# Order of small matmuls, two transposed blocks and the closing normalization in a one-core block kernel

## Chip, cores and metric

The kernel runs on one core of one Trainium2 chip. The metric is the device time of one execution in microseconds (us), as a median of several runs. The engines are TensorE (PE in the profile, PEld for its weight loads), VectorE (DVE), ScalarE (ACT), GpSimd (POOL) and SyncE (SP, which issues most DMAs). Data lies in SBUF, matmul results in PSUM, inputs and scratch in DRAM.

## What is computed

One layer of a network on 256 tokens of width 2048, in fp32: a feed-forward stage, a mixer and a second feed-forward stage, each between two normalizations and added to the running value. The mixer is the part that matters here:

```python
def _hybrid_mixer(u, w_in, ...):
    p = u @ w_in
    z_a, z_b, g_a, g_b = jnp.split(p, IN_SPLITS, axis=-1)
    y_a = _rwkv7_branch(z_a, ...) @ w_proj_a
    y_b = _pool_branch(z_b, pool_w, pool_scale) @ w_proj_b
    m = jax.nn.sigmoid(g_a) * y_a + jax.nn.sigmoid(g_b) * y_b
    return m @ w_out

def reference(x, ...):
    h = x
    f = _swiglu(_rmsnorm(h, ln_ffn1_pre[l]), ffn1_gate[l], ffn1_up[l], ffn1_down[l])
    h = h + MACARON_WEIGHT * _rmsnorm(f, ln_ffn1_post[l])
    mx = _hybrid_mixer(_rmsnorm(h, ln_mix_pre[l]), w_in[l], ...)
    h = h + _rmsnorm(mx, ln_mix_post[l])
    f = _swiglu(_rmsnorm(h, ln_ffn2_pre[l]), ffn2_gate[l], ffn2_up[l], ffn2_down[l])
    h = h + MACARON_WEIGHT * _rmsnorm(f, ln_ffn2_post[l])
    return h
```

`_rwkv7_branch` is a recurrence over the 256 tokens with 16 heads of 64. The kernel computes it in four chunks of 64 tokens for each half of the heads.

## The kernel before

**Products.** A product is done with the 256 tokens as two halves of 128 rows and 512 columns of the weight at a time (a block). Each fp32 factor is split into a high part H (rounded by ScalarE) and a low part L (the rest, by VectorE); a product is three matmuls of 128x128 by 512 columns (`mm3`): H·H, H·L and L·H. Weights come by DMA into `w32`, and are split into `wH` and `wL`, five buffers each. The activations must lie with their width along the partitions, so a result of one product is transposed before the next: `transpose_split` does it with four TensorE transposes of 128x128 for each half and block (tile `tr`), cast by ScalarE into `xH` and subtracted by VectorE into `xL`. The feed-forward stages use another way, `turn` and `carry`: VectorE turns 32x32 squares of the block into `T1`, SyncE writes `T1` to DRAM (`cx`), waits, and reads it back in four pieces with the squares put in their places (`x32`); the split then reads `x32`.

**The order.** Every operation is first recorded by `Plan`, with a cost. `simulate` then plays the five engines with these costs and writes out the order in which each engine gets its instructions. TensorE's operations belong to streams: `main` (the large products), `side` (transposes) and `chain` (the recurrence). At each step TensorE takes the first stream of chain, side, main whose next operation can go. The recurrence's matmuls are small and use the array in other shapes (64x128, 128x64, 64x64, 32x32); `cfg` tells the shape, and a change of it has a planned price (`SWITCH`). `deadlines` puts neighbouring chain operations of one shape into a `run`, and `whole` lets a run begin only when the operands of its first `RUN` = 16 operations are there and enough PSUM buffers are free; once begun, single operations of the run may go. All the results of chain and side share four PSUM buffers (`pt`). Results that matter: `pA` (products of AR and BK), `pB` (transposes of BK), then `pM`, `pX` and, for each chunk, `pU`, `pSa`, `pS`, `pY`; last `pg`.

**The mixer's end.** `MIX_ORDER` lists the main products; its last entries are the second half's recurrence `c1` and the gates `A0` to `A3`. The recurrence leaves `yT` (two halves, `yH` and `yL`). Then w_proj_a follows: `pairs` does the first two blocks of 512 columns together, first with the four row groups of the first half of `yT`, then with those of the second, in four PSUM banks; `gemm_tok` does the two others one by one. The evacuation `ev_pa` multiplies a block by its gate (`sga`), adds the other branch (`mb`, read back from DRAM) and calls `transpose_split` into `mT`. Then `down` does w_out, 2048 columns in two pairs of blocks f and l; some row groups (quads) are done by a scheme with seven products in place of eight, on the row groups of `mT[0]`. `OUT_QUADS` says how many quads, and after how many ordinary steps the first may come.

**The end of a stage.** `post` takes the four column blocks of the last product of a stage. For the last block (c = 3) and each half it makes the sum of squares (`sumsq`, ScalarE, tile `junk`), the factor of the normalization (`norm`: VectorE, then a power on GpSimd, tile `rs`), the product with the gain (`scale`, VectorE, tile `fg`), and then the four results. Sum of squares and product read the same PSUM buffer, and the planner does not let two engines read one buffer at once.

Of the kernel before, what the change touches and what calls it, by code (L numbers as in the profile page):

```python
# [15 lines left out]
ALU = mybir.AluOpType  # L16
# [10 lines left out]
NKW = W // P  # L27
# [16 lines left out]
AHEAD = 40000.0  # L44
EASE = 2.0
GATE_QUADS = [0, 0] + [3, 4] * 4 + [3]
OUT_QUADS = ((2, 2, 1.0), (2, 1, 1.0))
DOWN_QUADS = ((8, 1, 2.4), (8, 1, 1.7))
SCRATCH = 1024
SPARE = 1  # L50
HOLD = 3e5
Z_DMA = "k0 v0 k1 v1 r1"
POOL_DMA = [True, True]
MIX_ORDER = "p0 p1 l0 k0 m0 v0 m1 r0 m2 c0 B1 m3 k1 b0 b1 v1 r1 c1 B2 b2 B3 b3 A0 A1 A2 A3"
# [10 lines left out]


class TileInfo:
    __slots__ = ("tag", "left", "slot", "seq", "writes", "reads", "psum", "dl", "home", "lock")


class Engine:
# [10 lines left out]
LAND = 1600.0  # L82
SWITCH = 170.0
RUN = 16
TABLES = {AF.Exp: (0,), AF.Sigmoid: (2,), AF.Tanh: (0, 2, 18), AF.Silu: (18,)}
IN_ORDER = ("w32", "wH", "wL", "hH", "hL")


class Plan:

    def __init__(s, tc):
        s.tc, s.real = tc, tc.nc
        nc = s.real
        s.ops, s.tiles, s.tags, s.masks = [], {}, {}, {}
        s.order = {}
        s.shadow = bacc.Bacc("TRN2", target_bir_lowering=False, num_devices=1)
        s.clk, s.stream, s.lag, s.dl0 = 0.0, "main", 12000.0, None
        s.vector = Engine(s, "DVE", nc.vector)
        s.scalar = Engine(s, "ACT", nc.scalar)
        s.tensor = Engine(s, "PE", nc.tensor)  # L100
        s.gpsimd = Engine(s, "POOL", nc.gpsimd)
        s.sync = Engine(s, "SP", nc.sync)
# [8 lines left out]
    def tile(s, shape, dt, tag, name, pool, bufs):  # L111
        s.tags[tag] = bufs
        t = s.track(s.shadow.dram_tensor(name, tuple(shape), dt).ap(), tag)
        s.tiles[name].home = pool, list(shape), dt
        return t

    def region(s, ap):
# [32 lines left out]
    def add(s, eng, name, fn, a, k):  # L150
        o = Op()
        o.eng, o.fn, o.a, o.k = eng, fn, a, k
        o.i, o.nom, o.stream, o.lag = len(s.ops), s.clk, s.stream, s.lag
        o.preds, o.succs, o.tiles, o.new = set(), [], [], []
        aps = [(f"a{j}", x) for j, x in enumerate(a)] + list(k.items())
        aps = [(n, x) for n, x in aps if isinstance(x, bass.AP)]
        outs = [n for n, _ in aps if n in ("out", "accum_out")] or ["a0"]
        w = [x for n, x in aps if n in outs]
        r = [x for n, x in aps if n not in outs]
        if name == "memset":  # L160
            w, r = [a[0]], []
        s.cost(o, name, w, r, k)
        seen = set()
        for aplist, wr in ((r, False), (w, True)):
            for ap in aplist:
                g = s.region(ap)
                if g is None:
                    continue
                i, p0, p1, m = g
                if id(i) not in seen:  # L170
                    seen.add(id(i))
                    o.tiles.append(i)
                    i.left += 1
                for q0, q1, n, x, _ in i.writes:
                    if q0 < p1 and p0 < q1 and n & m and x is not o:
                        o.preds.add(x.i)
                if wr:
                    for q0, q1, n, x, _ in i.reads:
                        if q0 < p1 and p0 < q1 and n & m and x is not o:
                            o.preds.add(x.i)  # L180
                    for lst in (i.writes, i.reads):
                        lst[:] = [e for e in lst if not (p0 <= e[0] and e[1] <= p1
                                                         and e[2] & m == e[2])]
                    i.writes.append((p0, p1, m, o, None))
                else:
                    key = (p0, p1, m, eng, s.stream)
                    if eng == "PE":
                        i.reads[:] = [e for e in i.reads if e[4] != key]
                    i.reads.append((p0, p1, m, o, key))
        o.psum = [i for i in o.tiles if i.psum]  # L190
        s.ops.append(o)
        if eng == "PE" and s.stream == "main":
            s.clk += o.pace
        return o
# [46 lines left out]
    def deadlines(s):  # L241
        for o in s.ops:
            for p in o.preds:
                s.ops[p].succs.append(o)
        soon = {}
        for o in s.ops:
            if o.stream == "chain":
                soon[o.i] = max([soon[q] + s.ops[q].dur + SYNC for q in o.preds if q in soon
                                 and s.ops[q].nom == o.nom] or [0.0])
        idx, tip, run = {}, {}, []  # L250
        for o in s.ops:
            g = max([idx.get(q, -1) if s.ops[q].eng == "PE" else tip[q] for q in o.preds]
                    or [-1])
            tip[o.i] = g
            o.run = None
            if o.eng != "PE" or o.stream != "chain":
                continue
            idx[o.i] = len(idx)
            far = max([tip[q] for q in o.preds if s.ops[q].eng != "PE"] or [-1])
            if not run or run[-1].cfg != o.cfg or far >= idx[run[0].i]:  # L260
                run = []
            run.append(o)
            o.run = run
        for o in reversed(s.ops):
            d = o.nom + (0.0 if o.eng == "PE" else o.lag) + soon.get(o.i, 0.0) * EASE
            for x in o.succs:
                if o.eng == "PE" and x.eng == "PE":
                    continue
                e = x.dl - o.dur - SYNC - (2500 if o.nbytes else 0)
                if e < d:  # L270
                    d = e
            o.dl = d

    def simulate(s):
        s.deadlines()
        ops = s.ops
# [36 lines left out]
        def whole(o):  # L313
            if o.run is None or o.run is held:
                return True
            for x in o.run[:RUN]:
                for q in x.preds:
                    y = ops[q]
                    if y.eng != "PE" and (y.start is None or y.end + SYNC > now):
                        return False  # L320
            need = {id(i) for x in o.run[:RUN] for i in x.psum if i.slot is None}
            return len(need) <= len(slots["pt"])

        def go(o):
# [44 lines left out]
        while done < len(ops):  # L369
            moved = True  # L370
            while moved:
                moved = False
                for e in engines:
# [12 lines left out]
                    if e == "PE":  # L386
                        for st in rank:
                            q = streams[st]
                            if q and ready[q[0].i] and can(q[0]) and whole(q[0]):
                                held = q[0].run  # L390
                                go(q.popleft())
                                moved = True
                                break
                        continue
                    skipped = []
# [73 lines left out]
class Block:  # L469
# [272 lines left out]
            return x.rearrange("p (b k t) -> p k b t", k=4, t=32)  # L742
        return x.rearrange("p (i h k t) -> p k h i t", i=4, h=2, k=4)

    def carry(s, T1, T):
        v = s.carry_raw(T1)
        T.extend(s.new_T(1))
        for h in range(2):
            H, L = [t.rearrange("p k (h i t) -> p k h i t", h=2, i=4)[:, :, h] for t in T[-1]]
            s.split(v[:, :, h], H, L)  # L750

    def sumsq(s, src, acc):
# [139 lines left out]
class Kernel(Block):  # L892
# [156 lines left out]
    def post(s, gpost, fac, resid, emit, reload):  # L1049
# [10 lines left out]

        def norm(h, r):
            r2 = s.small(1, "rt2", bufs=2)
            nc.vector.tensor_scalar(out=r2, in0=ss[h][:, 3:4], scalar1=kf,
                                    scalar2=part[h], op0=ALU.mult, op1=ALU.add)
            nc.gpsimd.tensor_tensor(out=r, in0=r2, in1=s.mhalf[:, :1], op=ALU.pow)

        def ev(c, h, ps):
            if h == 0 and c % 2 == 0:
# [6 lines left out]
            if c == 3:  # L1075
                r = s.small(1, "rs", bufs=8)
                with s.set(lag=100.0):
                    s.sumsq(ps, ss[h][:, c:c + 1])
                    norm(h, r)
                    scale()  # L1080
                    for q in range(4):
                        o = cc_(fg[h], q)
                        nc.vector.scalar_tensor_tensor(out=o, in0=o, scalar=r,
                                                       in1=resid(h, q), op0=ALU.mult,
                                                       op1=ALU.add)
                        emit(h, q, o)
# [179 lines left out]
    def mixer(s, prm, uT, rs, resid, emit, gpost, reload):  # L1266
# [104 lines left out]
        mbs = {}  # L1371

        def ev_pa(c):
            def ev(h, ps):
                if h == 0:
                    mbs[c] = s.unit((P, 2, 512), F32, "mb")
# [1 line left out]
                sg = sga[c][:, h]  # L1378
                nc.vector.tensor_tensor(out=sg, in0=ps, in1=sg, op=ALU.mult)
                nc.vector.tensor_tensor(out=sg, in0=sg, in1=mbs[c][:, h], op=ALU.add)  # L1380
                s.transpose_split(sg, mT, c, h)
            return ev
        for x in MIX_ORDER.split():
            n = int(x[1])
# [10 lines left out]
                    chain(n)  # L1395
            else:
                {"B": gb_g, "b": pb_g, "A": ga_g}[x[0]](n)
        s.pairs(prm["w_proj_a"], (0, 512), at_a, NKW, 4, (ev_pa(0), ev_pa(1)))
        for c in range(2, 4):
            s.gemm_tok(prm["w_proj_a"], c * 512, at_a, NKW, ev_pa(c))  # L1400
        s.down(prm["w_out"], s.T_at(mT), NKD, s.post(gpost, 1.0, resid, emit, reload), mT,
               [], OUT_QUADS)
# [475 lines left out]
```

## Time and profile before

| | us |
|---|---|
| median of 3 runs | 2022.7 |
| lowest, highest | 2022.35, 2023.87 |
| the profiled execution, its own time | 2022.16 |
| its span, first to last instruction | 2020.2 |
| TensorE matmuls busy in it | 2002.1 |
| VectorE, ScalarE busy | 1750.4, 1185.9 |

The rows that the prediction shows are of three kinds. A row of the time order has the start in us from the beginning of the span, the length in us, the engine, the line of the code (455 for every operation, since a helper issues them all), the operation, the tile written, the tiles read, shapes and a count of equal instructions that follow each other; in brackets the idle time ahead of it and what ended it. A matmul's length is its time through the pipeline; matmuls start closer together than that. A small fp32 matmul of the chain stands as two in the trace. A row of the chain of waits has start, length and what the time went to. A row by groups has the count, the busy time, the mean in ns, and the idle time ahead.

### The profile page before, as it was taken

The page shows a single profiled execution, that of the slowest core. Times are in us where ns is not written, and L with a number is a line of the kernel's source. Part 1 is how long each engine was busy: PE and PEld are TensorE (multiplying, and loading weights), DVE is VectorE, ACT ScalarE, POOL GpSimd, SP SyncE. Part 2 cuts the span into 40 slices and gives each one's busy share as a digit, 9 for nine tenths or more (in the row PEclk, how much of TensorE's full clock was granted, in tenths as well). Part 3 has the DMA queues.
Part 4 walks back from the last instruction along what each step waited for, and adds up shares of the span by engine and source line. Part 5 has one row for each costly group of instructions (what it writes and reads, how often), then busy time and mean ns, then how long its engine had stood idle before and what let it go on. Part 6 is the DMA issues. An engine that isn't in the chain of part 4 may idle for free.

```text
span 2020.2 us, 28152 instructions
## 1 busy us (share of the span) xinstructions
PE 2002.1 (99%) x9835; PEld 1652.7 (82%) x9835; DVE 1750.4 (87%) x2284; ACT 1185.9 (59%) x1592; POOL 80.7 (4%) x148
## 2 busy tenths in 40 slices
PE   9999999999999999999999999999999999999998
PEld 7888888888888888887888788888888888788886
DVE  8999999999988758897868779798999999898885
ACT  7555656565555556764846455575555665655552
POOL 0000000000001110001200110010000000000000
PEclk9999999999999999999999999999999999999999
DMA  7788888886667677756475475667888888876673
GB/s 266 239 261 268 281 268 275 266 282 219 214 203 258 214 249 206 221 162 209 143 233 179 145 261 197 200 209 241 273 273 276 269 270 273 280 227 203 208 253 133
DMA packets 254054, 469.87 MB, mean 233 GB/s; under 512 B 20559, under 2 KB 42201, under 8 KB 253913
## 3 DMA queue, kind: packets, MB, share of 16 engines
q1 hardware_dynamic: 247737, 447.63, 68.5%
q0 software_dynamic: 5888, 19.93, 2.8%
q8 instruction: 77, 1.26, 0.3%
q14 instruction: 64, 0.52, 0.1%
q10 hardware_dynamic: 288, 0.52, 0.1%
HBM read 444.40 MB, written 23.59 MB: 232 GB/s over the span
## 4 chain that ended last, share of the span: by engine, by line
PE 79%; DVE 9%; DMA 6%; issue 3%; ACT 2%; SPq 1%; DVEq 0%; ACTq 0%; POOLq 0%
PE l L455 26%; PE f L455 23%; PE mm L455 22%; PE p L455 5%; DVE wL L455 4%; DMA w<-in_ffn_gate_dram 2%; DMA x<-cx 2%; DVE t L455 1%; ACT wH L455 1%; SPq L455 1%; DMA w<-in_ffn_up_dram 1%; PE tr L455 1%; DVE w L455 0%; PE pY L455 0%; DMA x<-in_x_dram 0%
## 5 line engine op out<-in xcount | busy, mean ns | idle before, releaser
L455 ACT CAST wH<-w 128x1024 fp32r<-128x1024 f32 (+2 forms) x722 | 746.7, 1046 | 632.4 <-DVE w L455 170.8
L455 DVE TENSOR_TENSOR wL<-w,wH 128x1024 fp32r<-128x1024 f32 (+2 forms) x722 | 863.2, 1210 | 167.6 <-ACT wH L455 163.4
L455 PE MATMUL l<-wL,xH 128*128 128x512 f32 x784 | 305.7, 390 | 0.8 <-DVE wL L455 0.7
L455 PE MATMUL l<-wH,xH 128*128 128x512 f32 x784 | 305.4, 390 | 0.0
L455 PE MATMUL l<-wH,xL 128*128 128x512 f32 x784 | 305.3, 389 | 0.0
L455 PE MATMUL mm<-wL,xH 128*128 128x512 f32 (+1 forms) x672 | 261.6, 389 | 0.0
L455 PE MATMUL mm<-wH,xH 128*128 128x512 f32 (+1 forms) x672 | 261.1, 389 | 0.0
L455 PE MATMUL mm<-wH,xL 128*128 128x512 f32 (+1 forms) x672 | 260.7, 388 | 0.0
L455 PE MATMUL f<-wH,xH 128*128 128x512 f32 x664 | 258.5, 389 | 0.0
L455 PE MATMUL f<-wL,xH 128*128 128x512 f32 x664 | 258.4, 389 | 0.0
L455 PE MATMUL f<-wH,xL 128*128 128x512 f32 x664 | 258.4, 389 | 0.0
L455 DVE TENSOR_TENSOR t<-w,w 128x1024 f32<-128x1024 f32 (+1 forms) x160 | 162.1, 1013 | 14.6 <-DMA w<-in_ffn_down_dram 8.0
L455 PEld LDWEIGHTS l<-wL,xH 128*128 128x128 f32 x784 | 147.2, 188 | 32.5 <-DVE wL L455 2.2
L455 PEld LDWEIGHTS l<-wH,xH 128*128 128x128 f32 x784 | 147.2, 188 | 30.6
L455 PEld LDWEIGHTS l<-wH,xL 128*128 128x128 f32 x784 | 147.2, 188 | 30.1
L455 PEld LDWEIGHTS mm<-wL,xH 128*128 128x128 f32 x672 | 126.4, 188 | 25.2 <-DVE wL L455 0.4
L455 PEld LDWEIGHTS mm<-wH,xH 128*128 128x128 f32 x672 | 126.3, 188 | 24.9
L455 PEld LDWEIGHTS mm<-wH,xL 128*128 128x128 f32 x672 | 126.2, 188 | 24.8 <-DVE xL L455 0.4
L455 PEld LDWEIGHTS f<-wH,xH 128*128 128x128 f32 x664 | 124.6, 188 | 26.0
L455 PEld LDWEIGHTS f<-wL,xH 128*128 128x128 f32 x664 | 124.6, 188 | 25.9
L455 PEld LDWEIGHTS f<-wH,xL 128*128 128x128 f32 x664 | 124.6, 188 | 25.8
L455 DVE TENSOR_TENSOR wL<-t,wH 128x1024 fp32r<-128x1024 f32 x98 | 119.0, 1214 | 3.0 <-ACT wH L455 2.8
(307 smaller groups left out, 2697.4 us busy)
## 6 DMA issues: line engine op xcount, KB each, us to landing
w<-in_w_in_dram SPq DMA_DIRECT2D x128, 512.0 KB
w<-in_ffn_up_dram SPq DMA_DIRECT2D x114, 512.0 KB
w<-in_ffn_gate_dram SPq DMA_DIRECT2D x112, 512.0 KB
w<-in_ffn_down_dram SPq DMA_DIRECT2D x112, 512.0 KB
w<-in_ffn_gate_dram SPq DMA_DIRECT2D x190, 256.0 KB
w<-in_ffn_up_dram SPq DMA_DIRECT2D x186, 256.0 KB
w<-in_ffn_down_dram SPq DMA_DIRECT2D x128, 256.0 KB
cx<-T SPq DMA_DIRECT2D x29, 512.0 KB
```

The costliest lines, as they stand in the source:

```text
L455: ins = o.fn(*[real(x) for x in o.a], **{n: real(x) for n, x in o.k.items()})
```

## The change

Four edits. In the planner, a run ends after 16 operations or when the kind of the result (the name of the PSUM tile) changes, `whole` asks for the whole run, and a new function `soon` makes TensorE hold back other work while the array is in a small shape and the next run of the chain can start within `STAY` = 400 planned ns. In the mixer, the first two blocks of w_proj_a are turned by VectorE and carried through DRAM instead of being transposed by TensorE; the four blocks are done one by one, without `pairs`; and w_out's first quad comes one step later. In `post`, the product of the last block is recorded as following the first step of `norm`, so the sum of squares comes first.

```diff
-OUT_QUADS = ((2, 2, 1.0), (2, 1, 1.0))
+OUT_QUADS = ((2, 3, 1.0), (2, 1, 1.0))
+MIX_DMA = 2
+STAY = 400.0
@@ Plan.add
+        if s.behind is not None:
+            o.preds.add(s.behind.i)
@@ Plan.deadlines
-            if not run or run[-1].cfg != o.cfg or far >= idx[run[0].i]:
+            if not run or run[-1].cfg != o.cfg or far >= idx[run[0].i] or len(run) == RUN \
+                    or run[-1].psum[0].kind != o.psum[0].kind:
                 run = []
@@ Plan.simulate
-            for x in o.run[:RUN]:
+            for x in o.run:
...
+        def soon(o):
+            for x in o.run or [o]:
+                for q in x.preds:
+                    y = ops[q]
+                    if y.eng != "PE" and (y.start is None or y.end + 305.0 > now + STAY):
+                        return False
+            need = {id(i) for x in o.run or [o] for i in x.psum if i.slot is None}
             return len(need) <= len(slots["pt"])
...
+                            if q and st == "chain" and cfg != (0, 0) and can(q[0]) and soon(q[0]):
+                                break
@@ Kernel.post
-                    norm(h, r)
-                    scale()
+                    with s.set(behind=norm(h, r)):
+                        scale()
@@ Kernel.mixer, ev_pa
-                s.transpose_split(sg, mT, c, h)
+                if c >= MIX_DMA:
+                    s.transpose_split(sg, mT, c, h)
+                    return
+                if not h:
+                    T1.append(s.unit(p="T1"))
+                s.turn(T1[0], h, sg)
+                if h:
+                    s.carry(T1[0], mT, c)
@@ Kernel.mixer
-        s.pairs(prm["w_proj_a"], (0, 512), at_a, NKW, 4, (ev_pa(0), ev_pa(1)))
-        for c in range(2, 4):
+        for c in range(4):
             s.gemm_tok(prm["w_proj_a"], c * 512, at_a, NKW, ev_pa(c))
```

`norm` returns its first VectorE instruction, a tile keeps its kind (its name without the number), and `carry` takes the place in `mT` into which it writes.

More of the change, by code (lines that the diff above doesn't have):

```diff
@@ L67 @@
 class TileInfo:
-    __slots__ = ("tag", "left", "slot", "seq", "writes", "reads", "psum", "dl", "home", "lock")
+    __slots__ = ("tag", "left", "slot", "seq", "writes", "reads", "psum", "dl", "home", "lock", "kind")
 class Engine:
@@ L96, in __init__ @@
         s.shadow = bacc.Bacc("TRN2", target_bir_lowering=False, num_devices=1)
-        s.clk, s.stream, s.lag, s.dl0 = 0.0, "main", 12000.0, None
+        s.clk, s.stream, s.lag, s.behind = 0.0, "main", 12000.0, None
         s.vector = Engine(s, "DVE", nc.vector)
@@ L114, in tile @@
         s.tiles[name].home = pool, list(shape), dt
+        s.tiles[name].kind = name.rsplit("_", 1)[0]
         return t
@@ L320, in whole @@
                         return False
-            need = {id(i) for x in o.run[:RUN] for i in x.psum if i.slot is None}
+            need = {id(i) for x in o.run for i in x.psum if i.slot is None}
+            return len(need) <= len(slots["pt"])
+        def soon(o):
[5 more added lines that the diff above has]
+            need = {id(i) for x in o.run or [o] for i in x.psum if i.slot is None}
             return len(need) <= len(slots["pt"])
@@ L743, in carry_raw, with carry @@
         return x.rearrange("p (i h k t) -> p k h i t", i=4, h=2, k=4)
-    def carry(s, T1, T):
+    def carry(s, T1, T, j=None):
         v = s.carry_raw(T1)
-        T.extend(s.new_T(1))
+        if j is None:
+            T.extend(s.new_T(1))
+            j = -1
         for h in range(2):
-            H, L = [t.rearrange("p k (h i t) -> p k h i t", h=2, i=4)[:, :, h] for t in T[-1]]
+            H, L = [t.rearrange("p k (h i t) -> p k h i t", h=2, i=4)[:, :, h] for t in T[j]]
             s.split(v[:, :, h], H, L)
@@ L1062, in norm @@
             r2 = s.small(1, "rt2", bufs=2)
-            nc.vector.tensor_scalar(out=r2, in0=ss[h][:, 3:4], scalar1=kf,
-                                    scalar2=part[h], op0=ALU.mult, op1=ALU.add)
+            o = nc.vector.tensor_scalar(out=r2, in0=ss[h][:, 3:4], scalar1=kf,
+                                        scalar2=part[h], op0=ALU.mult, op1=ALU.add)
             nc.gpsimd.tensor_tensor(out=r, in0=r2, in1=s.mhalf[:, :1], op=ALU.pow)
+            return o
         def ev(c, h, ps):
@@ L1373, in ev_pa @@
         def ev_pa(c):
+            T1 = []
             def ev(h, ps):
```

## The prediction

> **What bounds the kernel now.** I read the page first, then the chain of waits, then the time order of each engine where the changed lines run.
>
> ```profile
> span 2020.2 us, 28152 instructions
> PE 2002.1 (99%) x9835; PEld 1652.7 (82%) x9835; DVE 1750.4 (87%) x2284; ACT 1185.9 (59%) x1592; POOL 80.7 (4%) x148
> PEclk9999999999999999999999999999999999999999
> PE 79%; DVE 9%; DMA 6%; issue 3%; ACT 2%; SPq 1%; DVEq 0%; ACTq 0%; POOLq 0%
> 1973.03 38.09 PE l L455 x168
> 1186.00:1234.00 48.00, 48.00 (x225) 39.89 (x224) 37.75 (x47) 23.94 (x27) 1.06 (x2) 1.00 0.66 233
> ```
>
> TensorE is busy 99% at full clock. The fifth line, from the chain of waits, gives its pace: 38.09 us for 168 matmuls of 512 columns, 0.2267 us each. The last line, from the table by windows, covers w_proj_a: in 48 us TensorE is never idle (columns: window, length, busy time and count for PE, weight load, VectorE, ScalarE, GpSimd, then clock, DMA share, GB/s). So a microsecond counts only where TensorE issues less, changes its array shape less, or waits less; and at the end, where TensorE has finished. Work taken off the other engines is worth nothing by itself. The profiled execution took 2022.16 us (span and 1.96 us around it); the median of the three runs is 2022.7, 0.54 above.
>
> **Part 1: runs kept whole.** In the changed program's issue order TensorE changes to or from the full 128x128 array 74 times, before 82: four excursions fewer, all at pA and pB of the two chains. Time order of TensorE, second chain, then three rows of the first:
>
> ```profile
> 1072.69 0.39 PE L455 MATMUL mm<-wH,xH 128*128 128x512 f32 x1
> 1073.01 2.10 PE L455 MATMUL pA<-AR,BK 64*128 64x128 f32 x32
> 1075.04 0.50 PE L455 MATMUL mm<-wL,xH 128*128 128x512 f32 x1
> 1075.38 0.40 PE L455 MATMUL mm<-wH,xL 128*128 128x512 f32 x1
> ...
> 1077.89 0.39 PE L455 MATMUL mm<-wL,xH 128*128 128x512 f32 x1
> ...
> 1079.45 0.40 PE L455 MATMUL mm<-wH,xH 128*128 128x512 f32 x1
> 1080.10 0.68 PE L455 MATMUL pB<-ident,BK 64*128 64x64 f32 x15 [0.25 <-DVE AR L455]
> ...
> 1081.64 0.50 PE L455 MATMUL mm<-wH,xL 128*128 128x512 f32 x1
> 1082.18 2.02 PE L455 MATMUL pA<-AR,BK 64*128 64x128 f32 x30
> ...
> 1085.85 0.39 PE L455 MATMUL mm<-wL,xH 128*128 128x512 f32 x1
> 1086.17 0.80 PE L455 MATMUL pB<-ident,BK 64*128 64x64 f32 x16
> ...
> 1087.24 0.39 PE L455 MATMUL mm<-wH,xH 128*128 128x512 f32 x1
> ```
>
> ```profile
> 881.41 0.39 PE L455 MATMUL mm<-wL,xH 128*128 128x512 f32 x1
> ...
> 882.71 0.70 PE L455 MATMUL pB<-ident,BK 64*128 64x64 f32 x15
> ...
> 889.81 0.28 PE L455 MATMUL mc<-mxT,wH 128*128 128x256 f32 x1
> ```
>
> Whole runs have a price in these rows: pA from 1072.69 to 1075.38, less two matmuls, 2.24 us; pB from 1085.85 to 1087.24, less two matmuls, 0.94. A pB, pA, pB sequence of whole runs is 4.12. The second chain spent 9.35 us on it (1077.89 to 1087.24) with 17 matmuls (3.85) among them: 5.50, so 1.38 too much. The first spent 8.40 (881.41 to 889.81) with 11 matmuls (2.49): 5.91, 1.79 too much. Upper bound of the part: 3.17.
>
> Not all of that goes. Part of it is waiting for PSUM buffers: pB's 15 at 1080.10 start 0.65 us after the matmul of 1079.45, released by VectorE's AR. The changed order puts 19 matmuls between the first pA and pB, where 13 and 5 stood. They end near 1075.04 + 0.11 + 19 x 0.2267 = 1079.46, the switch takes 0.12, and the buffer is free near 1080.05: 0.45 of waiting stays. In the first chain 57 matmuls stand where 55 and 1 stood. They end near 882.1, against 882.71 for the second buffer: 0.5 stays. The gap ahead of pA (0.54 between 1081.64 and 1082.18, and the like ahead of its first piece) has 7 to 8 matmuls ahead of it now, which cover the evacuations. I take 3.17 - 0.95 = 2.2 saved; bounds 1.0 (all waits of more than a switch come back) and 3.2. The new rule that lets TensorE hold for up to 400 planned ns shows nowhere else in the issue order.
>
> **Part 2: two of four blocks turned by VectorE.** It removes four groups of four transposes from TensorE, with their ScalarE casts and VectorE subtractions from PSUM; it adds four VectorE turns, two writes to DRAM, eight reads of 128 KB and the same casts and subtractions from SBUF. TensorE, time order:
>
> ```profile
> 1210.90 0.39 PE L455 MATMUL mm<-wL,yH 128*128 128x512 f32 x1
> 1211.13 0.60 PE L455 MATMUL tr<-ident,sga 128*128 128x128 f32 x4
> ...
> 1212.48 0.39 PE L455 MATMUL mm<-wL,yH 128*128 128x512 f32 x1
> ```
>
> From 1210.90 to 1212.48 stand three matmuls and two groups: 1.58 - 0.68 = 0.90 us for one block. Two blocks: 1.81 saved.
>
> What could take it back is the carry. SyncE's issue of a write to DRAM and ScalarE's first cast of the block read back, the slowest and the fastest of the 22 such trips of the two feed-forward stages; and VectorE's prices:
>
> ```profile
> 360.98 0.33 SPq L455 DMA_DIRECT2D cx<-T  x1
> 373.51 1.14 ACT L455 CAST xH<-x 128x512 fp32r<-128x512 f32 x2 [3.06 <-DMA x<-cx]
> 1784.80 0.33 SPq L455 DMA_DIRECT2D cx<-T  x1
> 1795.17 0.62 ACT L455 CAST xH<-x 128x512 fp32r<-128x512 f32 x1 [0.69 <-DMA x<-cx]
> 1173.36 0.67 DVE L455 STREAM_TRANSPOSE yx<-yn 128x512 f32<-128x512 f32 x1
> 1202.66 1.28 DVE L455 TENSOR_TENSOR sga<-mm,sga 128x512 f32<-128x512 f32 x2
> L455 DVE TENSOR_TENSOR wL<-w,wH 128x1024 fp32r<-128x1024 f32 (+2 forms) x722 | 863.2, 1210 | 167.6 <-ACT wH L455 163.4
> ```
>
> A trip takes 10.4 to 12.5 us. Count from the start of w_proj_a's first block; a block is 48 matmuls, 10.88 us. Block 0: two products, two sums and two turns of some 0.6 end at 14.5, the cast starts at 24.9 to 27.0. Now it is VectorE's order that decides. Ahead of the sums that block 2's transposes need stand, in the changed order, two subtractions of the carried block (1.2), three wL (3.5, by the group's mean of 1.21 less what overlaps), the sum and one step of the quad operands (1.6) and three operations on sga (1.8), 8.1 in all, the first 0.6 after the cast: done at 33.6 to 35.7. TensorE comes to these transposes nine matmuls after block 2's end, at 34.7. It waits 0 to 1.0; I take 0.4, and for the range 0 and 1.5, since SyncE's reads also stand behind a weight load that waits for VectorE. Behind the transposes TensorE's whole queue waits.
>
> Block 1's carry: 21.8 + 3.6 + 10.4 to 12.5, and 2.5 for casts and subtractions, 38.3 to 40.4. w_out's first matmul, which reads this block, comes at 44.4 (four blocks and two groups of transposes). Slack 4 us, so nothing. While SyncE waits for that write, w_out's quad loads stand behind it, but they are wanted only after three pairs of 12 matmuls more (52 us).
>
> The blocks, no longer paired, need the second chain's result after one half block instead of two. The end of that chain on TensorE, and its last result on VectorE:
>
> ```profile
> 1169.49 0.28 PE L455 MATMUL pg<-lgs,kH 128*128 128x256 f32 x1
> 1184.20 0.68 DVE L455 TENSOR_TENSOR yL<-qb,yH 128x512 fp32r<-128x512 f32 x1
> ```
>
> Before, this last yL ended at 1184.88, 15.2 us after TensorE's pg run; now it is wanted after 66 + 24 matmuls, 20.4 us. On GpSimd's queue the loads mb<-msp of blocks 0 and 1 now stand ahead of some of the chain's copies; the 5 us cover that. Nothing there either.
>
> [...]
>
> **Part 3: square sum before the product.** The end of the run, after TensorE's last matmul:
>
> ```profile
> 2011.14 0.69 DVE L455 TENSOR_TENSOR fg<-l,gb 128x512 f32<-128x512 f32 x1 [5.74 <-PE l L455]
> 2011.87 0.60 ACT L455 ACTIVATE junk<-l 128x512 bf16<-128x512 f32 x1 [10.19 <-DVE fg L455]
> 2012.95 0.55 POOL L455 TENSOR_TENSOR rs<-rt,mhalf 128x1 f32<-128x1 f32 x1 [10.31 <-DVE rt L455]
> 2013.53 2.74 DVE L455 SCALAR_TENSOR_TENSOR fg<-fg,rs,h 128x512 f32<-128x512 f32 x4 [0.73 <-POOL rs L455]
> ```
>
> Both read one PSUM buffer and go one after the other. With the square sum first, ScalarE starts 0.73 earlier (2011.87 to 2011.14), and the product (0.69) fits in VectorE's 0.73 of waiting for GpSimd's power. Saved 0.73; bounds 0.5 and 0.75. At the two inner ends TensorE has other matmuls: nothing.
>
> **Sum.** 2022.16 - 2.2 - 1.81 + 0.4 - 0.73 = 2017.8 in the profiled execution's terms, with 0.54 to the median 2018.3; I round to 2018.2. In the last 2953 TensorE instructions (the second feed-forward) the order is the same, so that stage only shifts.
>
> **The rivals.**
> Waits come back: the whole runs save only 1.0, the transposes' wait is 1.5, the end 0.5: 0.8 in all, 2021.9; half-way, 2.5 saved, 2020.2. For it: the planner's times chose the old splits too, and TensorE still waited there. Against: what is kept is what the rows show.
> More goes than counted: pA/pB without any wait (3.2), no wait at the transposes, and some waits among the chains' small matmuls: 2016.5. The rows do not show why these should go.
> The carry is late (slower): block 0's subtractions stand in VectorE's queue ahead of block 2's sums, so beyond the 0.4, each microsecond of lateness is one of idle TensorE. Break-even is 4.5 us later than counted, a trip of 16; at 20 us the time is 2026. Against: 22 trips, the longest 12.5. [...]
> The change does nothing: runs split as before. The issue order excludes it for parts 2 and 3.
>
> **How the numbers follow.** 0.2% is 4.0 us, about what a measurement of this kernel can tell from no change. Forecast (2017 to 2019.5): 0.55, some of it above 2018.7, the line of 0.2%. Waits back, 2019.5 to 2022: 0.24. More goes, under 2017: 0.13. Late carry: 0.08. Faster 0.55, same 0.37, slower 0.08. Range 2015.6 to 2021.8.
>
> **What would show it.** Right: pA and pB as four runs each chain, with 0.3 to 0.6 us ahead of pB and none ahead of pA; tr<-ident,sga 16 in place of 32; four more turns of sga; ScalarE's last junk right behind the last l. Wrong: idle TensorE ahead of tr<-ident,sga, released by VectorE's sga, over 1.5 us; a wait of w_out's first f on xH or xL; longer waits ahead of pA; or a second feed-forward whose DMA waits have changed.

## The result, and the profile after

The changed kernel takes 2031.49 us (median of 6 runs, 2029.70 to 2034.77) beside 2022.53 us of the kernel before (6 runs): a ratio of 1.0043, 95% interval 1.0032 to 1.0054. It is slower by some 9 us, outside the predicted range. The profiled execution took 2031.16 us.

From the page of the changed kernel: span, busy time per engine, TensorE's busy slices and granted clock.

```profile
span 2029.1 us, 28147 instructions
PE 2001.3 (99%) x9819; PEld 1653.4 (81%) x9819; DVE 1752.5 (86%) x2288; ACT 1186.8 (58%) x1592; POOL 82.0 (4%) x148
...
PE   9999999999999999999999998999999999999998
...
PEclk9999999999999999999999998999999999999999
```

TensorE's work is there as predicted (16 transposes fewer), but one slice of the forty has an 8, in TensorE's row and in that of the clock. The windows of that place (48 us of w_proj_a, then the idle time and the 8 us behind it; columns as in the prediction's first fence):

```profile
1186.00:1234.00 48.00, 38.52 (x169) 31.81 (x168) 30.56 (x38) 17.01 (x20) 2.65 (x5) 0.91 0.82 245
```

```profile
1221.62:1231.49 9.87, 0.39 (x3) 0.03 (x1) 8.20 (x11) 3.98 (x5) 0.00 (x0) 0.69 0.63 204
1231.49:1233.49 2.00, 2.00 (x9) 1.82 (x10) 1.85 (x3) 0.59 (x1) 0.00 (x0) 0.50 1.04 251
1233.49:1235.49 2.00, 2.00 (x7) 1.61 (x6) 1.12 (x2) 1.33 (x2) 0.00 (x0) 0.50 0.99 356
1235.49:1237.49 2.00, 2.00 (x10) 1.65 (x9) 1.67 (x2) 1.35 (x3) 0.00 (x0) 0.95 0.29 110
```

Where the same 48 us of before had no idle time and full clock, TensorE now stands still for 9.48 us and then runs for 4 us at half its clock: 0.50 x 4 + 0.05 x 2 = 2.1 us lost on top. The order of events, rows picked from the time order of SyncE, GpSimd, ScalarE, VectorE and TensorE (start, length, engine, operation; in brackets the idle time before it and what ended it):

```profile
1187.74 0.53 POOL L472 DMA_DIRECT2D h<-hsp  x1 [11.80 <-PE mm L472]
1200.68 0.53 POOL L472 DMA_DIRECT2D h<-hsp  x1 [12.42 <-DVE sga L472]
1201.58 0.34 SPq L472 DMA_DIRECT2D cx<-T  x1
1201.90 0.53 POOL L472 DMA_DIRECT2D h<-hsp  x1 [0.69 <-DVE T L472]
1207.70 0.53 POOL L472 DMA_DIRECT2D h<-hsp  x1 [5.26 <-ACT wH L472]
1211.53 0.53 POOL L472 DMA_DIRECT2D gb<-in_ln_mix_post_dram  x1 [3.30 <-DVE sga L472]
1222.60 1.14 ACT L472 CAST xH<-x 128x512 fp32r<-128x512 f32 x2 [8.72 <-DMA x<-cx]
1223.25 1.29 DVE L472 TENSOR_TENSOR xL<-x,xH 128x512 fp32r<-128x512 f32 x2 [9.81 <-ACT xH L472]
1230.66 1.28 DVE L472 TENSOR_TENSOR sga<-sga,mb 128x512 f32<-128x512 f32 x2
1231.49 1.09 PE L472 MATMUL tr<-ident,sga 128*128 128x128 f32 x4 [9.48 <-DVE sga L472]
```

Block 0's trip, from SyncE's cx<-T to ScalarE's first cast, takes 1222.60 - 1201.58 = 21.0 us. ScalarE waits for it 8.72 us, VectorE for ScalarE 9.81, and block 2's sums and TensorE stand behind. From 0.9 us before the write on (1200.68 to 1211.53), GpSimd issues three loads of h and one of gb, 512 KB each. Most of the length is in the reads: SyncE issues the first of them at 1207.13, 5.6 us after the write, and from there to the cast it is 15.5 us. In the trace before, the same five loads came earlier, when nothing was carried:

```profile
1181.54 0.53 POOL L455 DMA_DIRECT2D h<-hsp  x1 [8.68 <-PE mm L455]
...
1187.89 0.53 POOL L455 DMA_DIRECT2D gb<-in_ln_mix_post_dram  x1 [0.38 <-issue]
```

They wait for free buffers of the kind `u`. The carry takes such buffers too (`T1` and `x32`), so the loads' buffers now come free with sga and T, that is with the carry itself.

Cutting the span at the first matmul of each stage, and taking from each stage 0.2267 us for each of its 512-column matmuls, leaves the time that is not matmul pace (us; the second table has the other kernels of the study, in the stages that are used below):

```
stage                        before  after  p1_only p2_only order  late   mid0   mid1
first feed-forward            15.33  13.86   19.21   15.46  16.27  13.98  15.17  17.68
mixer to first pA             26.20  27.24   26.70   26.53  27.12  26.53  27.11  28.52
first pA to first pM          10.55   9.49    9.49   10.58   9.42   9.44   9.44   9.46
first pM to first pg's end    21.17  22.17   22.13   23.03  23.54  22.10  25.18  24.04
to second pA                   4.92   6.15    6.13    4.91   6.13   6.10   6.11   6.10
second pA to second pM         8.97   9.09    9.42    9.79   8.70   9.25   8.69   8.67
to second pg's end            19.94  19.60   19.59   19.96  19.63  19.58  19.59  19.64
w_proj_a to w_out's first f    2.79  12.57    2.79   11.49   0.95   1.36   7.90   2.55
w_out to second feed-forward   2.76   2.73    2.76    2.74  10.18   2.88   2.75   8.19
second feed-forward            4.79   4.15    3.86    8.61   4.52   2.74   4.72   2.41
behind the last matmul         9.52   8.74    9.53    9.39   8.67   8.66   8.78   8.76

stage                        half   p3_only carry_late nostay three early_b
first pA to first pM           9.47  10.57   10.59      9.47   9.45   9.45
first pM to first pg's end    21.27  22.62   24.89     23.37  23.80  22.41
to second pA                   6.15   4.91    4.91      6.15   6.11   6.14
second pA to second pM         8.29   9.04    8.97      8.69   8.73   8.74
to second pg's end            19.67  20.00   19.97     19.61  19.65  20.25
w_proj_a to w_out's first f    1.33   2.83    1.79      2.79   0.00   5.25
w_out to second feed-forward   3.00   2.76    2.88      2.78   4.71   2.74
behind the last matmul         8.67   8.80    8.85      9.52   9.05   8.67
```

Of the 8.84 us by which after exceeds before over all stages, w_proj_a holds 9.78 and the end -0.78; the rest cancels. The first feed-forward differs by up to 5.4 us between these traces without an edit that aims at it, so the argument goes by the stages where the waits lie and not by the spans of single traces.

### The profile page after: what moved, and what is told of

It is laid out like the page before. It is cut to its first block, busy times and chain, and to the rows that moved or that the text cites. A ratio compares the mean times of both kernels' runs of the same rounds, so it can differ in the third digit from the quotient of the medians.

```text
span 2029.1 us, 28147 instructions
## 1 busy us (share of the span) xinstructions
PE 2001.3 (99%) x9819; PEld 1653.4 (81%) x9819; DVE 1752.5 (86%) x2288; ACT 1186.8 (58%) x1592; POOL 82.0 (4%) x148
## 4 chain that ended last, share of the span: by engine, by line
PE 69%; DVE 10%; issue 9%; DMA 7%; ACT 4%; SPq 1%; POOL 0%; DVEq 0%; ACTq 0%; POOLq 0%
PE l L472 25%; PE f L472 22%; PE mm L472 16%; DVE wL L472 5%; PE p L472 4%; DMA w<-in_ffn_gate_dram 3%; DMA x<-cx 2%; ACT wH L472 1%; DMA w<-in_ffn_up_dram 1%; DVE t L472 1%; SPq L472 1%; DMA cx<-T 0%; DVE w L472 0%; DVE xL L472 0%; DVE T L472 0%
```

## The experiments

Theories. (1) The trip is long because GpSimd's loads, moved into it, share the DMA engines with it. (2) The trip is long in this place by itself: SyncE's queue, the weights' loads. (3) A long trip does harm only because VectorE's order puts the carried block's splits ahead of block 2's sums. And for the planner's part: it brings the predicted 2.2 us, or its gain is lost elsewhere in the recurrence.

**p1_only: the planner's edits alone.** The carry and the end are as before:

```diff
-MIX_DMA = 2
+MIX_DMA = 0
-                    with s.set(behind=norm(h, r)):
-                        scale()
+                    norm(h, r)
+                    scale()
```

(with `pairs` and the old `OUT_QUADS` back).

> The planner's runs kept whole alone; the two blocks are turned by TensorE as before, the product stands before the square sum as before. By the prediction's first part (2.2 us of excursions saved, bounds 1.0 to 3.2): 2020.3 us, 2019.3 to 2021.5. By the rival read from the stages of the changed kernel (0.9 us won in the stretches of pA and pB, 2 to 3 us lost at longer waits of pS, pk and Z elsewhere in the recurrence): 2022.5 to 2024.5, with the idle time ahead of pS<-Z at 2 us or more (1.1 before).

Ratio 0.9999, 0.9989 to 1.0009: worth nothing that can be measured, not 2.2 us. The stages say why, since the kernels with the old planner and those with the new one agree among themselves. From first pA to pM 10.55 to 10.59 become 9.42 to 9.49, 1.1 won; up to the second pA 4.91 to 4.92 become 6.10 to 6.15, 1.2 lost. The rows of p1_only for that loss (time order of ScalarE, VectorE, TensorE):

```profile
1012.43 2.50 ACT L472 COPY od<-vt 32x512 f32<-32x512 f32 x4
1015.02 0.69 DVE L472 COPY nb<-n 128x1024 f32<-128x1024 f32 x1 [2.60 <-issue]
1015.77 1.09 PE L472 MATMUL pk<-ident,nb 128*128 128x128 f32 x8 [1.18 <-DVE nb L472]
```

VectorE's nb starts as soon as ScalarE's last copy of vt ends (1014.93), so TensorE waits 1.18 us at pk. In the trace before, nb came 14.5 us ahead of that copy's end (990.88, 1005.33) and pk waited for nothing. So it is in the traces of all the kernels: nb and pk well ahead of the last copy with the old planner, right behind it with the new one. That vt's buffer is what nb waits for is read from the times only. The longer wait of pS<-Z named in the expectation is not the planner's: the stage from pM to pg is 21.2 to 24.9 with the old order and 21.3 to 25.2 with the new.

**p2_only: the carry alone.**

> The carry alone, with the planner and the end as before. All theories of the loss put it here: TensorE idle 8 to 11 us ahead of block 2's transposes, the first trip (issue of cx<-T to the cast xH<-x) 19 to 23 us, about 2031 to 2034 us. If the loss hung on the planner's new order, the first trip would be under 14 us, and the time under 2024.

1.0052, 1.0034 to 1.0069. TensorE's wait at block 2's transposes, from its time order:

```profile
1232.78 1.09 PE L460 MATMUL tr<-ident,sga 128*128 128x128 f32 x4 [8.12 <-DVE sga L460]
```

The first trip is 1204.18 to 1223.89, 19.7 us. The loss sits in the carry, whatever the planner does.

**order: the splits of the carried blocks behind block 2's sums.**

```diff
+                    if h and c == MIX_DMA:
+                        with s.set(behind=o):
+                            for j in range(MIX_DMA):
+                                s.place(raws[j], mT[j])
...
-                    s.carry(T1[0], mT, c)
+                    raws.append(s.carry_raw(T1[0]))
```

(`o` is block 2's last sum, `place` the two splits that `carry` made.)

> The changed kernel with the splits of the two carried blocks recorded behind block 2's sums on VectorE and ScalarE; nothing else moved. Theory that the order is the cost (a slow trip hurts only because block 2's sums stand behind it): idle ahead of block 2's transposes under 1.5 us although the first trip still takes 19 to 23 us, and a wait of 0 to 3 us ahead of w_out's first products instead; 2020 to 2024 us. If the carried blocks are needed just as early by w_out, the idle time only moves there: 6 to 10 us ahead of w_out's f, 2028 to 2032.

1.0006, 0.9991 to 1.0020: neither of the two answers, since block 2's transposes no longer wait and w_out's first f does not wait either. But two later places do, from the time order of ScalarE and TensorE and the windows behind the first:

```profile
1225.15 1.13 ACT L472 CAST xH<-x 128x512 fp32r<-128x512 f32 x2
...
1231.51 0.62 ACT L472 CAST xH<-x 128x512 fp32r<-128x512 f32 x1 [4.25 <-DMA x<-cx]
...
1240.79 1.11 PE L472 MATMUL tr<-ident,sga 128*128 128x128 f32 x4 [3.30 <-DVE sga L472]
...
1253.28 0.47 PE L472 MATMUL p<-wH,sH 128*128 128x512 f32 x1 [1.09 <-DVE xL L472]
```

```profile
1240.79:1244.79 4.00, 4.00 (x14) 3.43 (x15) 3.30 (x7) 2.16 (x4) 0.00 (x0) 0.50 0.02 7
1244.79:1248.79 4.00, 4.00 (x16) 3.25 (x15) 4.00 (x4) 1.95 (x2) 0.00 (x0) 0.81 0.40 131
```

3.30 + 1.09 and 0.50 x 4 + 0.19 x 4 = 2.8 us of clock: 7.2 of the 7.4 by which w_out's stage grew. The first cast starts 20.4 us after the write (1204.78), but here it stands behind block 2's sums (done at 1225.19) and waits for no data, so 20.4 is only an upper bound of the trip. The wait has moved to block 1's cast, 4.25 us, and block 3's sums stand behind its splits. Theory 3 explains a part: w_proj_a and w_out together have 11.13 us over the matmuls' pace here, 15.30 in the changed kernel and 5.55 before.

**late: GpSimd's loads of h held until block 3's sums.** A small copy on GpSimd that nothing reads waits for these sums, and the loads follow it:

```diff
+        def later():
+            o = nc.gpsimd.tensor_copy(s.rtmp("lt"), sga[3][:, 1, :256])
+            with s.set(behind=o):
+                reload()
-        ... s.post(gpost, 1.0, resid, emit, reload), mT,
+        ... s.post(gpost, 1.0, resid, emit, later), mT,
```

> The changed kernel with GpSimd's four loads of h back (2 MB) held until block 3's sums are done; the order of everything else as in the changed kernel. Theory that the carry shares the DMA engines with these loads: DMA share in the 20 us after the first cx<-T falls from 0.8 to 1.1 to 0.4 to 0.6, the first trip takes 10 to 13 us, idle ahead of block 2's transposes at most 1.5 us, 2020 to 2022.5 us. Rival that the trip is slow by itself here (SP's queue, the weights' loads): trip 18 us or more, 2028 or more. A third outcome is that the loads of h then come late for the second feed-forward: a new wait of some us there.

0.9993, 0.9981 to 1.0005; the profiled span is 2015.9, of the fastest of the ten executions. Time order of the engines:

```profile
1200.94 0.34 SPq L472 DMA_DIRECT2D cx<-T  x1
1212.71 1.14 ACT L472 CAST xH<-x 128x512 fp32r<-128x512 f32 x2 [0.45 <-DMA x<-cx]
1221.60 0.63 PE L472 MATMUL tr<-ident,sga 128*128 128x128 f32 x4 [0.23 <-DVE sga L472]
1239.62 2.08 POOL L472 DMA_DIRECT2D h<-hsp  x4
```

The trip is 11.8 us, of which 6.9 lie behind SyncE's first read (1205.85), the wait is 0.23, and nothing new waits behind. Through w_proj_a the orders of all engines but GpSimd are those of the changed kernel, so theory 2 falls. One expectation missed: the DMA share does not fall to 0.4 to 0.6.

```profile
1206.00:1209.00 3.00, 3.00 (x15) 2.47 (x14) 2.15 (x3) 1.33 (x2) 0.00 (x0) 1.00 1.01 316
1209.00:1212.00 3.00, 3.00 (x15) 2.49 (x14) 3.00 (x6) 1.34 (x2) 0.00 (x0) 1.00 1.04 262
```

The DMA engines are just as full, now with SyncE's weights, and the trip is short all the same. What differs is whose transfers fill them. The queues' view, of the changed kernel from 1201 to 1223 us and of late from 1201 to 1213 (packets, MB, share of 16 engines):

```profile
q1 hardware_dynamic: 2086, 3.88, 57.9%
q0 software_dynamic: 576, 2.10, 34.3%
```

```profile
q1 hardware_dynamic: 1861, 3.33, 90.1%
```

q0 carries GpSimd's loads (late, where GpSimd issues none in this time, has no such row), q1 what SyncE issues, the carry among it. With q0 at work, q1 moves 3.88 MB in 22 us; alone, it moves 3.33 in 12. How the DMA engines divide their time between q0 and q1, no run here shows.

**half: three of the four loads held.** As late, with `reload` split in two and its second half behind the copy. The plan put the second load behind the copy as well, so that one load stays early (1186.26) and three are held, and it is no half dose.

> The changed kernel with only the last two of GpSimd's four loads of h back (1 MB of 2) held until block 3's sums are done; the other two stay where the changed kernel has them. If the trip is long by the bytes that share the DMA engines, it lies between that with all four held (11.8 us) and that with none held (21.0 us): 14 to 18 us, TensorE idle 2 to 6 us ahead of block 2's transposes, 2022 to 2028 us. If a part of the loads decides alone, it is at one end: under 13 us with an idle time under 1 us, or over 19.

0.9975, 0.9964 to 0.9987: the first trip is 11.7 us, the wait 0.20. The load at 1186 had landed before the carry began, so this is nearly late once more, and it tells nothing of a dose.

**mid0 and mid1: the same loads, at two other moments.** Only the sums that GpSimd's copy waits for differ from late; the other engines' orders through w_proj_a are the same:

```diff
-            o = nc.gpsimd.tensor_copy(s.rtmp("lt"), sga[3][:, 1, :256])
+            o = nc.gpsimd.tensor_copy(s.rtmp("lt"), sga[0][:, 1, :256])   (mid1: sga[1])
```

> The run with GpSimd's loads of h held, but its small copy waits for block 0's sums instead of block 3's: every engine's order is the same, only the moment differs at which the loads (0.5 MB of gain, then 2 MB of h) are issued, about 1203.5 us on, on top of block 0's carry. If the loads in flight make the trip long: first trip 17 to 21 us (11.8 with the loads held), TensorE idle 5 to 9 us ahead of block 2's transposes and its clock at half behind that; 2026 to 2032 us. If it was the changed place of something else in the changed kernel: trip under 13 us, idle under 1 us, 2020 to 2023.

> The same with the copy waiting for block 1's sums: the loads are issued from about 1214.5 us, on top of block 1's carry and behind block 0's. If loads in flight make a trip long: block 0's stays at 11 to 13 us and TensorE isn't late at block 2's transposes, block 1's grows from 14 us (1211.8 to 1225.4 with the loads held) to 18 to 23, and since VectorE's splits of block 1 stand ahead of block 3's sums the wait moves to block 3's transposes: 2 to 7 us idle there, 2022 to 2028 us. If the loads don't matter: both trips as with the loads held, 2020 to 2023.

mid0: 1.0023, 1.0011 to 1.0035. Time order:

```profile
1204.66 0.53 POOL L472 DMA_DIRECT2D gb<-in_ln_mix_post_dram  x1 [0.18 <-issue]
1205.20 0.53 POOL L472 DMA_DIRECT2D h<-hsp  x1
1205.25 0.34 SPq L472 DMA_DIRECT2D cx<-T  x1
1222.26 1.15 ACT L472 CAST xH<-x 128x512 fp32r<-128x512 f32 x2 [5.69 <-DMA x<-cx]
1231.15 1.08 PE L472 MATMUL tr<-ident,sga 128*128 128x128 f32 x4 [5.48 <-DVE sga L472]
```

mid1: 1.0022, 1.0007 to 1.0037:

```profile
1208.09 0.34 SPq L472 DMA_DIRECT2D cx<-T  x1
1218.88 2.13 POOL L472 DMA_DIRECT2D h<-hsp  x4
1218.90 0.34 SPq L472 DMA_DIRECT2D cx<-T  x1
1221.05 1.14 ACT L472 CAST xH<-x 128x512 fp32r<-128x512 f32 x2 [1.64 <-DMA x<-cx]
1237.74 1.14 ACT L472 CAST xH<-x 128x512 fp32r<-128x512 f32 x2 [4.92 <-DMA x<-cx]
1245.96 1.12 PE L472 MATMUL tr<-ident,sga 128*128 128x128 f32 x4 [3.78 <-DVE sga L472]
```

With the loads on block 0's carry its trip is 17.0 us and TensorE idles at block 2's transposes, 5.48. With the loads on block 1's carry, block 0's trip is 13.0 and block 1's 18.8 (1218.90 to 1237.74); TensorE idles 1.43 at block 2's transposes, a little more than expected, and 3.78 at block 3's. The idle time goes where the loads go. So it is shown that GpSimd's loads in flight make the trip long. That they do it at the DMA engines, and not elsewhere on the way to DRAM, is argued from the queues' shares; no run has the same loads on SyncE's queue.

**early_b: the loads ahead of the carry.**

```diff
+        reload()
         for c in range(4):
             s.gemm_tok(prm["w_proj_a"], c * 512, at_a, NKW, ev_pa(c))
```

(and no `reload` in w_out's `post`.)

> The other direction: the changed kernel with the four loads of h recorded ahead of w_proj_a's first block instead of at w_out's first sums, so that they take their buffers and are issued before the carry (three of them in the second chain). If the loads in flight are what makes the trip long: first trip 10 to 13 us, under 0.5 us of idle time ahead of block 2's transposes, the stretch from w_proj_a to w_out's f 1.2 to 1.5 us shorter than before, ratio 0.997 to 0.9995. If it only matters that GpSimd's queue does something near the carry: as the changed kernel, 1.003 to 1.005. A third outcome: the loads delay the second chain's own trips, and 1 to 3 us are lost at its waits.

1.0009, 1.0000 to 1.0018: neither end of what was expected. The four loads of h are gone from the carry (issued from 1089.63 to 1136.45), but the load of gb, which I had not moved, stays in it:

```profile
1202.09 0.34 SPq L472 DMA_DIRECT2D cx<-T  x1
1205.41 0.53 POOL L472 DMA_DIRECT2D gb<-in_ln_mix_post_dram  x1 [32.97 <-DMA cx<-T]
1216.19 1.14 ACT L472 CAST xH<-x 128x512 fp32r<-128x512 f32 x2 [2.74 <-DMA x<-cx]
1225.09 0.66 PE L472 MATMUL tr<-ident,sga 128*128 128x128 f32 x4 [2.53 <-DVE sga L472]
```

This is the dose that half failed to give. With nothing on GpSimd's queue during the trip it takes 11.8 us (late); with 0.5 MB 14.1 (early_b); with 2 MB 21.0 (after). TensorE's idle time goes 0.23, 2.53, 9.48. In these three that is 2.3 us for each 0.5 MB, but the price is not a constant: in mid0 the queues' view has 2.19 MB on q0 from 1205 to 1223, as much as in the changed kernel, and the trip takes 17.0, 1.2 us for each 0.5 MB. Block 1's trip in mid1 is 5.1 us longer than in late, with 2.6 MB. More bytes on q0 came with a longer trip in the first three (11.8, 14.1, 21.0 us); what else sets the price is open. early_b's order differs from the changed kernel's in the second chain as well.

**p3_only, carry_late, nostay, three.** The square sum alone; late with the old planner; the planner's part without the hold:

```diff
-                            if q and st == "chain" and cfg != (0, 0) and can(q[0]) and soon(q[0]):
-                                break
```

and late with `MIX_DMA = 3`.

> The square sum ahead of the product alone, everything else as before. By the prediction's third part the stretch behind the last matmul is 0.5 to 0.75 us shorter (9.52 before), and nothing else: ratio 0.9996, which the timing can't tell from no change; the stretch in the profile can.

0.9993, 0.9983 to 1.0002; the stretch behind the last matmul is 8.80 against 9.52, 0.72 less.

> The carry with the loads of h back held until block 3's sums, and the end's new order, with the planner as before (runs cut as before). If the runs kept whole are worth nothing, as their run alone says (0.9999), the same as with them: 2.2 us under before by the stages (1.4 at w_proj_a, 0.8 at the end), ratio 0.9985 to 0.9995. If they are worth the 2.2 us predicted, it is 2 us over the run that has all three parts and the held loads: ratio 1.000 to 1.001.

0.9992, 0.9980 to 1.0005, the same as with the planner's part (late, 0.9993). So is w_proj_a's stage but for 0.4 us.

> The planner's runs kept whole, but without the rule that TensorE waits for a chain's product which will be ready within 400 ns; the carry and the end as before. If that rule brings the gain of the stretch from pA to pM (9.5 us of overhead against 10.6 before) it is back at 10.5 here; if it brings the loss of the stretch from pg to the second pA (6.1 against 4.9, with a wait of 1.2 us of pk for VectorE's nb) that is back at 4.9. Time within 0.2% of before in either case.

0.9997, 0.9988 to 1.0006: both stretches stay at their new values (9.47 and 6.15), so neither answer was right. The hold decides neither; the whole runs bring the gain and the loss.

> Three blocks instead of two carried through DRAM, with the loads of h held until block 3's sums. If the carry is free where nothing shares the DMA engines, it saves another 0.9 us of transposes: ratio 0.998 to 0.9995. If block 2's trip (issued about 1224, landed about 1236, then 2.5 us of splits) is late for w_out, TensorE waits some us in w_out's first part: ratio 1.000 to 1.003.

0.9987, 0.9973 to 1.0000. w_proj_a's stage is 1.36 shorter than in late, w_out's 1.83 longer, since block 3's transposes now stand behind w_out's first f, with short waits of these (0.75) and of p for xL: no gain over two blocks.

Whether late, half, carry_late and three differ from each other can't be told by their intervals. Of the twelve kernels half alone has an interval wholly below 1. Its first trip and waits are those of late, whose interval reaches 1.0005, so a gain of the repaired kernel over the one before is likely but not settled.

## Why the prediction was wrong, point by point

**The failed step** is the trip's price in part 2, "a trip takes 10.4 to 12.5 us". The 22 trips behind it were of other stages, and I did not ask what else would be on the DMA engines in this one. Of GpSimd's queue I looked at mb's loads alone and put it at nothing ("Nothing there either"). The reload of h, which waits for `u` buffers that the carry now takes, moved into the carry unseen. In place of 12.5 at most stood 21.0; with GpSimd's loads elsewhere the same trip is 11.8.

**The rest of part 2's working held.** Block 0's turns were counted to end 14.5 us after w_proj_a's start; SyncE issued the write 14.4 after it (1187.17 to 1201.58). From the cast to the end of what block 2's transposes need: 8.7 counted (0.6 + 8.1), 8.9 measured (1222.60 to 1231.49). Put 21.0 for the trip and this sum gives 44.2 us against TensorE's 34.7, the 9.5 us seen. And with the trip as I had it, late saves 2.79 - 1.36 = 1.43 at w_proj_a where I had 1.81 - 0.4 = 1.41. (With the old planner, in carry_late, it is 1.00, with a wait of 0.68.) But late as a whole, 0.9993, is 1.4 us below before (3.8 below to 1.0 above) and not the 4.3 of the forecast's terms: part 1 was off too.

**The rival "the carry is late"** named place, mechanism and releaser, and the sign for a wrong forecast (idle TensorE ahead of tr<-ident,sga, released by sga, over 1.5 us) is the one that came. Its chance of 0.08 rested on the longest of 22 trips, all of other stages, so they could not bound this one. Its price was too low as well: 2026 for a trip of 20. A microsecond of lateness costs more than one of idle TensorE: here 9.48 idle and 2.1 of half clock.

**Block 1's carry**, counted as free by 4 us: in the changed kernel its cast came 22.9 us after the write (1212.80 to 1235.70), hidden by the idle time already there. That is no slow transfer alone: SyncE issued its reads only 14.5 us after the write, behind w_out's weight loads, and the cast waited for no data. In mid1, where it alone is late, it costs 3.78 idle and some 1.5 of clock.

**Part 1** was mis-sized: 2.2 forecast, bounds from 1.0. At pA and pB the first chain saved 1.1 of 1.79 and the second about 0.4 of 1.38 (means of 9.2 with the old planner, 8.8 with the new); a further 0.36 came in the second chain's later stage, and 1.2 went at pk, because the order that changed was not that of pA and pB alone: nb and pk moved behind vt's copies. By the stages some 0.6 is left; by the timing 0.2, give or take 2. The bound from below had no term for a new wait elsewhere in the chain.

**Part 3** was right: 0.73 forecast, 0.72 alone and 0.78 in the changed kernel. Its rows after:

```profile
2020.78 0.60 ACT L472 ACTIVATE junk<-l 128x512 bf16<-128x512 f32 x1 [10.19 <-PE l L472]
2021.63 0.68 DVE L472 TENSOR_TENSOR fg<-l,gb 128x512 f32<-128x512 f32 x1
2022.45 2.74 DVE L472 SCALAR_TENSOR_TENSOR fg<-fg,rs,h 128x512 f32<-128x512 f32 x4
```

The product fits between the square sum and the last step, as counted.

**Sums of the prediction.** The rival "waits come back" saves 1.8 us by its own terms (1.0 + 1.81 - 1.5 + 0.5), not 0.8: 2020.9, so the upper end of the range, 2021.8, stood 1 us too high. The forecast adds up to 2018.4, not 2018.2. The lower end, 2015.6, has no working. None of this reaches 2031.

## What to carry to other kernels

The price of a transfer taken from another stage holds only with the same company (here 11.8 us without GpSimd's loads, 21.0 with them): list what every queue issues in the new place, and where loads wait for buffers of a shared pool, ask what a new user of that pool does to the moment at which they start. Moving such loads out of the way brought more here, by the stages, than reordering the work behind them, which moved most of the wait to the next block (w_proj_a and w_out together: 15.30 us over the matmuls' pace in the changed kernel, 4.24 in late, 11.13 in order). And where TensorE sets the time, an idle stretch of some microseconds is to be priced with the clock behind it (here 2.1 us behind 9.48, 2.8 behind order's 3.30).

## What was not expected of the hardware

**Half clock behind idle time.** All six idle stretches of TensorE of 3.3 us and more, in all these runs, were followed by 2.8 to 5.5 us of half clock (3.30, 3.32, 3.78, 5.48, 8.12, 9.48). Of twelve between 2.1 and 3.0 us six were, mostly the longer ones, but 2.12 in nostay was and 2.70 in p2_only was not. Outside the first 40 us, none between 1 and 2 us was (1.18 at pk in p1_only and 1.43 in mid1 among them). Windows of two of the twelve, nostay's behind its wait of 2.12 us and p2_only's behind its 2.70:

```profile
951.75:953.75 2.00, 2.00 (x38) 1.88 (x40) 1.08 (x3) 0.00 (x0) 0.80 (x2) 0.58 0.02 8
```

```profile
952.41:954.41 2.00, 2.00 (x48) 1.82 (x48) 1.25 (x3) 0.00 (x0) 0.79 (x2) 1.00 0.00 0
```

So the length of the idle time alone does not decide: 2.12 us were enough in nostay (a clock of 0.58 in the first window), 2.70 in p2_only were not (1.00). Nor does half clock begin when TensorE starts again. In the changed kernel it lasts 10.24 us, from 1225.44 to 1235.68, and the first 6.05 of them lie in the idle time. By the windows it lasts 6.8 us in order (behind 3.30 us of idle time), and 3.4 in mid0 (behind 5.48), early_b (2.53) and nostay (2.12). What sets these lengths, and what decides whether the clock is halved, is not shown here.

**A full set of DMA engines was not the same as a slow trip.** At shares of 1.01 and 1.04 with SyncE's loads the carry took 11.8 us; with two queues at work and shares of 0.7 to 1.1 it took 21.0. The share of a window did not tell which queue waits.
